# One decoder layer on one core: other banks for the first projection, token tiles in pairs, a third gate buffer, spread compressed-branch steps

## The chip, the core and the metric

The kernel runs on one core of a Trainium2 chip. The metric is the device time of one execution in microseconds, here the median of three runs. The engines are named as in the profile: PE (TensorE, the matrix engine; PEld are its weight loads), DVE (VectorE), ACT (ScalarE), POOL (GpSimd) and SP (SyncE, which issues most DMAs here). The kernel names eight PSUM banks, in which TensorE adds up its products.

## What is computed

One layer of a hybrid decoder on x of 512 tokens by 1024 channels, in fp32. Cut to its frame:

```python
h = rms_norm(x, norm1_g)
u = h @ w_in                       # 11512 columns, split among what follows
(dq, dk, dv, iq, ik, iw, nq, nkv, ng, sz, sxbc, sdt, mg) = split(u)
y_a = dsa_mixer(norm(dq), norm(dk), dv, iq, ik, iw)   # attention to the 256 keys that an index picks
y_b = nsa_mixer(norm(nq), *nkv, sigmoid(ng), ...)     # compressed + selected + window attention
y_c = ssd_mixer(sz, sxbc, sdt, ...)                   # Mamba-2: conv, chunked scan, gated norm
gates = sigmoid(mg)                                   # three gates per channel
mix = gates[0] * (y_a @ w_br_dsa) + gates[1] * (y_b @ w_br_nsa) + gates[2] * (y_c @ w_br_ssd)
x = x + mix @ w_out
x = x + square(relu(rms_norm(x, norm2_g) @ w_ff1)) @ w_ff2
```

DSA scores every earlier key with a small index and keeps the best 256 by repeated MAX8 and MATCH_REPLACE rounds on VectorE. NSA has two key groups and three parts: 31 compressed blocks of the keys (whose probabilities also pick four blocks of 64 keys), the picked blocks, and the window.

## The kernel before

Every fp32 operand of a projection is split into a high and a low half in fp32r, and each product is three matmuls, high by high, high by low and low by high (`mm3`, L455 to L457). A weight block of 128 x 1024 goes through a pipeline (`WS`): a DMA into `wraw` (three buffers), ACT makes the high half `whi` (L172), and DVE or POOL subtracts it for the low half `wlo` (L174). The set `LOWP` says which of the numbered blocks take POOL; before, they are block 0 and blocks 8 to 23. Blocks 0 to 3 belong to the first projection, 4 to 11 to the NSA keys and values, 12 to 19 to the DSA queries.

Two generators share TensorE. `filler()` runs what is plain matmul: the first projection c0 (DSA key and value, index queries and keys, SSD time steps), nkv (two halves, 512 and 304 columns), the DSA queries dq, then z, x (with the conv), the NSA queries nq, 24 merge gates (each written to DRAM as `g_d`), then the branches a0, c0, c1, b0, b1, b2, then `w_out` and the feed-forward part. `main()` runs the mixers: the DSA index, DSA attention, the SSD, NSA. Each step of `main` yields a debt in time, and as much filler is put in behind it. The framework then lists the instructions of each engine by priority and by its own timeline, so the order that an engine runs is not that of the text. The engines run in order; an instruction waits for its semaphores, and all behind it on that engine wait too.

PSUM has eight banks: two named `pj` (projections), two `sc` (scores), two `pT` (transposes), one `pv`, one `pF`. A projection by token tile (`proj_tok`, L473) takes one `pj` bank for each of four tiles of 128 tokens, runs through the four weight blocks, and hands the bank to a callback `cb` that reads it out. For c0 (L695) the callback copies to `u0`, makes the value halves (`make_v`, L547 to L549, tile `v_d`) and the index queries `iqs`; for nkv (L730, L745) it makes `v_s` and `v_w` and copies the keys to `u1` and `u2`, from which `make_k` computes squares (`sqk`, L522), their sum (`stk`, L524), the power on POOL (`rtk`, L527) and the keys.

The SSD runs 16 units (four chunks by four groups). Each unit loads `E` and `xz` by DMA; POOL masks `E`, scales `xt`, `xw` and `xz`, adds `t` and decays the state `hst`; TensorE ends the unit with the transposes of `yv` (L1321), and `yev` is stored to DRAM as `yc_d`. The filler beside it is the conv projections x and then nq, whose queries are stored (`q_d`), and whose norm is a power on POOL (`rs`, L619, `mhalf` as exponent).

NSA has eight (block, group) pairs, and each has four attention steps: j = 0 and 1 by window (w) and selected (s). A step can load something for later. The compressed part of the next pair is done in three pieces (`cmp_a`, which loads the queries `qu` by DMA from POOL and computes the compressed scores at L1032, `cmp_b`, `cmp_c`), hung on the steps of the pair before: `cmp_a` on (0, w), `cmp_b` on (0, s), `cmp_c` on (1, s).

In `branches()` each output tile m of a branch has a gate tile `gld` (two buffers, L1393), loaded from `g_d` by SP, multiplied with the projection's bank (L1508) and added to `mixf` (L1511); in b2 `mixf` is then split into `mixh` and `mixl` (L1513, L1514). For the branches c the gate is first multiplied by a row of factors R (`rtok`). The inputs of a branch come from DRAM through a ring of two tiles (`yr`, L810) that the gates `gth` share, and are split into `yh` (L811) and `yl`.

## Time and profile before

| | |
|---|---|
| median of three runs | 1391.43 us (1391.18 to 1393.15) |
| the profiled execution | 1393.32 us, its span 1391.6 us |
| PE busy | 1361.1 us, 98% |
| PEld | 1134.0 us, 81% |
| DVE | 1002.0 us, 72% |
| ACT | 721.3 us, 52% |
| POOL | 282.0 us, 20% |
| mean granted TensorE clock | 0.994 |

The span is from the first to the last instruction of the profiled execution; the time around it is 1.7 us. Busy time is what an engine spends on instructions, idle time is put down to what released the next one. The granted clock is a share of 2.4 GHz, so 0.50 is 1.2 GHz. A matmul's printed length contains a tail that overlaps with the next one; the pace is read from the starts, or from a busy stretch by its count.

### The profile page before, as it was taken

How to read it: one execution, taken by the hardware profiler on the slowest of the kernel's cores; microseconds unless marked ns; L12 is line 12 of the kernel's file. 1: busy time of each engine (PE TensorE's matmuls, PEld its weight loads, DVE VectorE, ACT ScalarE, POOL GpSimd, SP SyncE). 2: the span in 40 equal slices, each digit the busy share in tenths (PEclk: the TensorE clock that was granted, in tenths of full speed). 3: DMA queues.
4: the chain of work that ended last, by engine and by line, in shares of the span. 5: the costliest groups of instructions: out<-in, count | busy, mean ns of one | idle time of the engine just before them, and what ended most of it. 6: DMA issues, size and time to landing. Idle time of an engine off the chain costs nothing.

```text
span 1391.6 us, 19651 instructions
## 1 busy us (share of the span) xinstructions
PE 1361.1 (98%) x6875; PEld 1134.0 (81%) x6875; DVE 1002.0 (72%) x1966; ACT 721.3 (52%) x1434; POOL 282.0 (20%) x231
## 2 busy tenths in 40 slices
PE   8989999999999999999999999999999999999998
PEld 7878888888877778788887888787889888888887
DVE  6599977999868666477667888878845576767841
ACT  5545336667766757356566564655324434343430
POOL 2345211110048485100000003123100101102000
PEclk9999999999999999999999999999999999999999
DMA  6335654644477696634434544535545665746531
GB/s 194 94 93 145 176 172 133 167 112 126 118 240 240 187 273 193 176 106 137 129 111 140 144 125 118 143 116 162 166 148 152 121 167 134 167 120 134 157 114 53
DMA packets 222592, 205.34 MB, mean 148 GB/s; under 512 B 15369, under 2 KB 169885, under 8 KB 222494
## 3 DMA queue, kind: packets, MB, share of 16 engines
q1 hardware_dynamic: 206524, 180.49, 44.2%
q0 software_dynamic: 15232, 20.98, 8.1%
q10 hardware_dynamic: 738, 2.63, 0.5%
q8 instruction: 54, 0.88, 0.3%
q14 instruction: 44, 0.36, 0.1%
HBM read 167.56 MB, written 36.51 MB: 147 GB/s over the span
## 4 chain that ended last, share of the span: by engine, by line
PE 69%; DVE 10%; DMA 8%; POOL 5%; issue 4%; ACT 3%; SPq 0%; ACTq 0%; POOLq 0%; DVEq 0%
PE pj L455 16%; PE pj L456 16%; PE pj L457 16%; PE sc L455 3%; PE sc L456 3%; PE sc L457 3%; PE pT L935 2%; DMA gld<-g_d 2%; PE sc L897 2%; PE sc L896 1%; DMA yr<-yc_d 1%; PE pv L948 1%; PE pv L947 1%; POOL mixf L1511 1%; DVE mask L867 1%
## 5 line engine op out<-in xcount | busy, mean ns | idle before, releaser
L172 ACT ACTIVATE whi<-wraw 128x1024 fp32r<-128x1024 f32 (+2 forms) x190 | 198.0, 1048 | 226.2 <-PE pj L456 115.5
L174 DVE TENSOR_TENSOR wlo<-wraw,whi 128x1024 fp32r<-128x1024 f32 (+1 forms) x173 | 217.4, 1261 | 101.5 <-ACT whi L172 99.5
L457 PE MATMUL pj<-hTh,wlo 128*128 128x512 f32 x384 | 154.0, 401 | 0.0
L455 PE MATMUL pj<-hTh,whi 128*128 128x512 f32 x384 | 153.5, 400 | 0.2 <-DVE cacc L828 0.2
L456 PE MATMUL pj<-hTl,whi 128*128 128x512 f32 x384 | 153.0, 398 | 0.0
L905 ACT ACTIVATE p<-p,nb,rs 128x256 f32<-128x256 f32 (+3 forms) x192 | 123.2, 645 | 56.2 <-DVE nb L903 56.1
L455 PE MATMUL pj<-whi,hTh 128*128 128x512 f32 (+2 forms) x352 | 138.2, 393 | 6.5 <-DVE stk L525 3.2
L456 PE MATMUL pj<-wlo,hTh 128*128 128x512 f32 (+2 forms) x352 | 138.1, 393 | 0.0
L457 PE MATMUL pj<-whi,hTl 128*128 128x512 f32 (+2 forms) x352 | 137.0, 390 | 0.0
L455 PE MATMUL pj<-yh,whi 128*128 128x512 f32 (+1 forms) x288 | 107.6, 377 | 3.3 <-ACT yh L811 2.3
L456 PE MATMUL pj<-yl,whi 128*128 128x512 f32 (+1 forms) x288 | 107.7, 374 | 0.0
L457 PE MATMUL pj<-yh,wlo 128*128 128x512 f32 (+1 forms) x288 | 107.6, 374 | 0.0
L456 PE MATMUL pj<-h2l,whi 128*128 128x512 f32 (+1 forms) x256 | 96.3, 376 | 0.0
L457 PE MATMUL pj<-h2h,wlo 128*128 128x512 f32 (+1 forms) x256 | 96.2, 376 | 0.0
L455 PE MATMUL pj<-h2h,whi 128*128 128x512 f32 (+1 forms) x256 | 96.1, 376 | 0.0
L991 POOL DMA_DIRECT2D qu<-q_d x32 | 23.6, 738 | 317.1 <-PE sc L897 212.3
L455 PEld LDWEIGHTS pj<-hTh,whi 128*128 128x128 f32 x384 | 72.7, 189 | 15.2 <-issue 1.1
L457 PEld LDWEIGHTS pj<-hTh,wlo 128*128 128x128 f32 x384 | 72.7, 189 | 14.8 <-issue 0.7
L456 PEld LDWEIGHTS pj<-hTl,whi 128*128 128x128 f32 x384 | 72.7, 189 | 13.8 <-issue 0.2
L455 PEld LDWEIGHTS pj<-whi,hTh 128*128 128x128 f32 x352 | 67.0, 190 | 20.5 <-issue 5.7
L939 ACT ACTIVATE pth<-pT 128x512 fp32r<-128x512 f32 x95 | 54.4, 593 | 52.0 <-PE pT L935 51.3
L457 PEld LDWEIGHTS pj<-whi,hTl 128*128 128x128 f32 x352 | 67.0, 190 | 13.1 <-issue 0.7
(385 smaller groups left out, 3280.7 us busy)
## 6 DMA issues: line engine op xcount, KB each, us to landing
wraw<-in_w_in_dram SPq DMA_DIRECT2D x84, 512.0 KB, 4.3
wraw<-in_w_ff_dram SPq DMA_DIRECT2D x58, 512.0 KB, 4.2
gld<-g_d SPq DMA_DIRECT2D x40, 256.0 KB, 2.7
qd<-in_w_ff_dram POOLq DMA_DIRECT2D x18, 512.0 KB, 6.0
q_d<-qev SPq DMA_DIRECT2D x64, 128.0 KB, 3.2
qu<-q_d POOLq DMA_DIRECT2D x32, 256.0 KB, 4.0
E<-ac_d SPq DMA_DIRECT2D x16, 512.0 KB, 5.8
xz<-xz_d SPq DMA_DIRECT2D x16, 512.0 KB, 4.9
```

Source lines behind the costliest of these rows:

```text
L172: act.activation(hi[:, :m], r[:, :m], AF.Copy)
L174: (pool if i in LOWP else dve).tensor_tensor(lo[:, :m], r[:, :m], f(hi[:, :m]), op=ALU.subtract)
L455: pe.matmul(o, lh, rh, start=first, stop=False)
L456: pe.matmul(o, lh, rl, start=False, stop=False)
L457: pe.matmul(o, ll, rh, start=False, stop=last)
L867: dve.scalar_tensor_tensor(wk, r[:, :n], iwt[:, b, h:h + 1], caus[:, 384 - 128 * b:] if h == 0 else wk, op0=ALU.mult, op1=ALU.add)
L896: pe.matmul(s_[:, h % w, :n], u.q[h], kh[:, :n], start=True, stop=False)
L897: pe.matmul(s_[:, h % w, :n], u.q[h], kl[:, :n], start=False, stop=True)
L905: act.activation(u.p[h][:, :n], u.p[h][:, :n], AF.Exp, bias=u.nb[:, h:h + 1], scale=rs8[:, u.b, u.h0 + h:u.h0 + h + 1], accum_out=u.sm[:, ...
L935: pe.transpose(pt[:, h], u.p[h][:, kb * 128:kb * 128 + 128], ident)
L939: act.activation(ph, ptf, AF.Copy)
L991: pool.dma_start(q.rearrange("p (i a) c -> p i (a c)", i=2), src)
```

## The change

Five edits:

- `LOWP` leaves out blocks 14 to 16, so that their low halves are made by DVE.
- `proj_tok` can take the token tiles in pairs: two tiles go through two weight blocks each before the next two blocks. Both halves of nkv use it; the first projection c0 stays with tile after tile, but takes the banks `pj`, `pj`, `sc`, `sc` for its four tiles.
- In NSA the queries of the next pair are loaded at (0, w), `cmp_a` moves to (0, s), `cmp_b` to (1, w), and `cmp_c` stays at (1, s). The mark `nsa0`, for which b0 waits, moves with `cmp_b`.
- In `branches` every third gate tile of the branches b takes the row R, which is not read any more by then, and loads are issued one or two tiles earlier.
- For the branches c the product of gate and R is issued after the first 12 of a tile's 24 matmuls, not ahead of them.

```diff
-LOWP = {0} | set(range(8, 24))
+LOWP = {0} | set(range(8, 14)) | set(range(17, 24))
...
-    def proj_tok(plan, lh, ll, cb):
+    def proj_tok(plan, lh, ll, cb, pair=False, tags=("pj",) * NB):
...
+        if pair:
+            seq = [(t, s) for t0 in (0, 2) for s0 in (0, 2) for t in (t0, t0 + 1) for s in (s0, s0 + 1)]
+        else:
+            seq = [(t, s) for t in range(NB) for s in range(4)]
+        acc = {}
+        for t, s in seq:
+            if s == 0:
+                acc[t] = ps(tags[t], [128, 512])
...
-        yield from proj_tok(P["c0"], hTh, hTl, cb0)
+        yield from proj_tok(P["c0"], hTh, hTl, cb0, False, ("pj", "pj", "sc", "sc"))
...
-            yield from proj_tok(P["nkv"][0], hTh, hTl, cb1)
+            yield from proj_tok(P["nkv"][0], hTh, hTl, cb1, True)
...
-            yield from proj_tok(P["nkv"][1], hTh, hTl, cb2)
+            yield from proj_tok(P["nkv"][1], hTh, hTl, cb2, True)
...
-            if i < len(order) and order[i] not in Q:
+            if i < len(order):
+                b, g = order[i]
+                load(i)
+                yield from cmp_a(b, g, Q[b, g], ratio)
...
+        def load(i):
+            if i < len(order):
                 b, g = order[i]
                 Q[b, g] = [load_q(4 + 2 * g + j, b) for j in range(2)]
-                yield from cmp_a(b, g, Q[b, g], ratio)
+            return iter(())
...
                     elif j == 0 and kind == "w":
-                        u.load = lambda i=i: start(i + 1)
+                        u.load = lambda i=i: load(i + 1)
...
                     if i and j == 0 and kind == "s":
+                        u.load = lambda i=i: cont(i + 1, cmp_q)
+                    if i and j == 1 and kind == "w":
                         u.load = lambda i=i: cont(i + 1, cmp_b)
-                    if i == 4 and j == 0 and kind == "s":
+                    if i == 4 and j == 1 and kind == "w":
                         u.load = lambda i=i: mark(cont(i + 1, cmp_b))
...
-                g_ = bp.tile([128, S], F32, name="gld", bufs=2)
+                if br[0] == "b":
+                    gcnt[0] += 1
+                g_ = R if br[0] == "b" and gcnt[0] % 3 == 0 else bp.tile([128, S], F32, name="gld", bufs=2)
...
                     load_g(8 * bi + m + 2)
+                    load_g(8 * bi + m + 4)
+                elif br == "b0":
+                    load_g(8 * bi + m + 2)
...
-                if br[0] == "c":
-                    dve.scalar_tensor_tensor(th, th, 1.0, R, op0=ALU.add, op1=ALU.mult)
...
-                        yield from proj_ch(P["br_" + br][m], lambda i: yh[i], lambda i: yl[i], p)
+                        for i_, v_ in enumerate(proj_ch(P["br_" + br][m], lambda i: yh[i], lambda i: yl[i], p)):
+                            yield v_
+                            if i_ == 1 and br[0] == "c":
+                                dve.scalar_tensor_tensor(th, th, 1.0, R, op0=ALU.add, op1=ALU.mult)
```

How many filler matmuls stand where follows from the two generators, so these edits move work on every engine. Three places of the emitted order follow.

PE in the first projection, before, from the last matmuls of tile t=1 (`pj`) to the first of t=2; L424 are transposes of x:

```order
L455 MATMUL pj<-whi,hTh 128x456
L456 MATMUL pj<-wlo,hTh 128x456
L457 MATMUL pj<-whi,hTl 128x456
L424 MATMUL pT<-ident,x_125 128x128 x8
L455 MATMUL pj<-whi,hTh 128x456
L456 MATMUL pj<-wlo,hTh 128x456
```

and after, the same place:

```order
L455 MATMUL pj<-whi,hTh 128x456
L456 MATMUL pj<-wlo,hTh 128x456
L457 MATMUL pj<-whi,hTl 128x456
L455 MATMUL sc<-whi,hTh 128x456
L456 MATMUL sc<-wlo,hTh 128x456
L424 MATMUL pT<-ident,x_125 128x128 x4
L457 MATMUL sc<-whi,hTl 128x456
```

The first matmuls of t=2 moved ahead of the transposes and write to a bank of `sc`.

DVE at the end of nkv's second half, before, from `v_w` of tile t=2 to that of t=3 (309 and 310 are the two key groups):

```order
L549 TENSOR_TENSOR v_w_310<-pj,v_w_310 128x64
L873 MATCH_REPLACE mask_628<-m_753,mask_628 128x256
L872 MAX m_762<-mask_628 128x8
L873 MATCH_REPLACE mask_628<-m_762,mask_628 128x256
L872 MAX m_771<-mask_628 128x8
L522 TENSOR_TENSOR sqk<-u_792 128x256
L755 TENSOR_SCALAR gate<-gate 128x192
L873 MATCH_REPLACE mask_628<-m_771,mask_628 128x256
L549 TENSOR_TENSOR v_w_309<-pj,v_w_309 128x64
```

and after:

```order
L879 MATCH_REPLACE mask_640<-m_748,mask_640 128x256
L555 TENSOR_TENSOR v_w_310<-pj,v_w_310 128x64
L174 TENSOR_TENSOR wlo<-wraw,whi 128x1024
L878 MAX m_762<-mask_640 128x8
L174 TENSOR_TENSOR wlo<-wraw,whi 128x1024
L528 TENSOR_TENSOR sqk<-u_786 128x256
L761 TENSOR_SCALAR gate<-gate 128x192
L555 TENSOR_TENSOR v_w_309<-pj,v_w_309 128x64
```

Two of the three subtractions that came over from POOL stand between the two, and fewer rounds of MAX and MATCH_REPLACE.

POOL from the end of the SSD to the first query loads of NSA, before (L1294 ends a unit's sum, L1358 is the SSD's norm, L619 the norm of a half of the queries):

```order
L1275 TENSOR_TENSOR xt<-xz,sv_dth 128x512
L1294 TENSOR_TENSOR t_5475<-t_5475,xz 128x512
L1282 TENSOR_TENSOR xz<-xz,dskip 128x512
L1294 TENSOR_TENSOR t_5541<-t_5541,xz 128x512
L1358 TENSOR_TENSOR rst<-sst,mhalf 128x4
L619 TENSOR_TENSOR rs_319<-ssq,mhalf 128x4x8
L991 DMA qu<-q_d_3_68 128x2x256 x2
```

and after:

```order
L1311 TENSOR_TENSOR t_5475<-t_5475,xz 128x512
L625 TENSOR_TENSOR rs_319<-ssq,mhalf 128x4x8
L1292 TENSOR_TENSOR xt<-xz,sv_dth 128x512
L1299 TENSOR_TENSOR xz<-xz,dskip 128x512
L1311 TENSOR_TENSOR t_5541<-t_5541,xz 128x512
L1375 TENSOR_TENSOR rst<-sst,mhalf 128x4
L997 DMA qu<-q_d_3_68 128x2x256 x2
L997 DMA qu<-q_d_0_65 128x2x256 x2
L625 TENSOR_TENSOR rs_319<-ssq,mhalf 128x4x8
L997 DMA qu<-q_d_2_67 128x2x256 x2
```

Both powers `rs` moved against their neighbours: the first now stands ahead of the last unit's `xt`, the second behind four query loads. The stretch from the SSD's first matmul to its last `yv` transpose holds 335 filler matmuls before and 239 after. By the intervals between the `yv` transposes of one unit and the next these are, before: 38 up to the first, then 13, 15, 11, 15, 14, 17, 24 (intervals 1 to 7), 70 (8), 14, 13, 18, 15 (9 to 12), 17, 17, 24; after: 41, then 8, 15, 10, 11, 13, 17, 13, then 21, then 5, 5, 8, 11, then 16, 21, 24. From there to the first compressed score stand 61 before and 40 after.

## Rows read from the trace of the kernel before

**Rows 1.** The page, part 1: busy us (share of the span) and instructions of each engine.
```profile
PE 1361.1 (98%) x6875; PEld 1134.0 (81%) x6875; DVE 1002.0 (72%) x1966; ACT 721.3 (52%) x1434; POOL 282.0 (20%) x231
```

**Rows 2.** Waits of PE: line and tile, releaser: us in total, times, longest.
```profile
PE pj L455 <- DVE stk L525: 3.2, 1, 3.2
...
PE pj L455 <- DVE gld L1508: 0.9, 3, 0.3
```

**Rows 3.** Stretches: length, busy us (count) by engine, granted clock, DMA share, GB/s.
```profile
core 0: us, PE busy (x) PEld busy (x) DVE busy (x) ACT busy (x) POOL busy (x), PEclk, DMA share, GB/s
27.58:30.99 3.41, 3.41 (x11) 2.97 (x10) 0.71 (x2) 0.00 (x0) 0.00 (x0) 0.50 0.37 99
75.00:100.00 25.00, 21.85 (x123) 19.08 (x122) 24.79 (x62) 12.29 (x28) 11.71 (x6) 1.00 0.30 86
398.70:553.10 154.40, 146.16 (x793) 116.23 (x791) 105.80 (x124) 104.22 (x281) 104.56 (x81) 0.99 0.76 234
417.80:477.00 59.20, 54.67 (x314) 43.80 (x312) 47.43 (x57) 40.76 (x120) 42.27 (x33) 1.00 0.74 226
497.60:530.00 32.40, 32.22 (x180) 25.01 (x179) 19.80 (x26) 19.22 (x57) 32.40 (x25) 1.00 0.90 276
740.00:760.00 20.00, 17.70 (x91) 14.99 (x90) 11.55 (x35) 10.62 (x23) 0.72 (x1) 0.91 0.58 171
935.00:965.00 30.00, 28.28 (x140) 22.36 (x139) 24.09 (x70) 17.74 (x40) 8.79 (x5) 1.00 0.47 144
1100.00:1375.00 275.00, 275.00 (x1215) 227.72 (x1214) 181.38 (x199) 108.27 (x120) 24.23 (x20) 1.00 0.56 137
```

**Rows 4.** PE's timeline at six waits: start, length, instruction, count, [idle before, releaser].
```profile
26.37 0.45 PE L455 MATMUL pj<-whi,hTh 128*128 128x456 f32 x1 [1.80 <-DVE v_d L549]
...
90.51 0.47 PE L455 MATMUL pj<-whi,hTh 128*128 128x512 f32 x1 [3.15 <-DVE stk L525]
...
569.79 0.30 PE L1032 MATMUL sc<-kc,qu 128*128 128x64 f32 x1 [1.33 <-DMA qu<-q_d]
...
753.28 0.73 PE L455 MATMUL pj<-yh,whi 128*128 128x512 f32 x2 [2.30 <-ACT yh L811]
...
885.54 0.63 PE L1032 MATMUL sc<-kc,qu 128*128 128x64 f32 x4 [1.50 <-DMA qu<-q_d]
...
1007.39 0.47 PE L455 MATMUL pj<-whi,mixh 128*128 128x512 f32 x1 [1.80 <-ACT mixh L1513]
```

**Rows 5.** DVE's timeline: a subtraction at 23.30, then 82.85 to 90.76.
```profile
23.30 1.22 DVE L174 TENSOR_TENSOR wlo<-wraw,whi 128x1024 fp32r<-128x1024 f32 x1
...
82.85 0.41 DVE L873 MATCH_REPLACE8 mask<-m,mask 128x256 f32<-128x256 f32 x1
83.29 0.43 DVE L872 MAX8 m<-mask 128x8 f32<-128x256 f32 x1
83.63 2.54 DVE L522 TENSOR_TENSOR sqk<-u 128x256 f32<-128x256 f32 x1
86.10 2.42 DVE L755 TENSOR_SCALAR gate<-gate 128x192 f32<-128x192 f32 x1
...
90.35 0.41 DVE L522 TENSOR_TENSOR sqk<-u 128x256 f32<-128x256 f32 x1
```

**Rows 6.** POOL's timeline: weights 14 to 16, then the SSD and its end.
```profile
81.11 7.29 POOL L174 TENSOR_TENSOR wlo<-wraw,whi 128x1024 fp32r<-128x1024 f32 x3 [7.95 <-ACT whi L172]
...
509.30 5.89 POOL L619 TENSOR_TENSOR rs<-ssq,mhalf 128x32 f32<-128x32 f32 x1
...
554.78 5.43 POOL L619 TENSOR_TENSOR rs<-ssq,mhalf 128x32 f32<-128x32 f32 x1
562.12 2.94 POOL L991 DMA_DIRECT2D qu<-q_d  x4 [1.91 <-ACT gth L776]
```

**Rows 7.** ACT's timeline ahead of the branch a0.
```profile
741.29 0.58 ACT L776 ACTIVATE gth<-pj 128x512 f32<-128x512 f32 x1
...
752.60 1.27 ACT L811 ACTIVATE yh<-yr 128x512 fp32r<-128x512 f32 x2 [4.55 <-DMA yr<-ya_d]
```

**Rows 8.** DVE's timeline at the last pair of b2.
```profile
1006.87 0.76 DVE L1508 SCALAR_TENSOR_TENSOR gld<-gld,pj 128x256 f32<-128x256 f32 x2 [0.36 <-DMA gld<-g_d]
```

More of the change, by code (lines that the diff above doesn't have):

```diff
@@ L472, in run_later @@
                 e[1]()
-    def proj_tok(plan, lh, ll, cb):
+    def proj_tok(plan, lh, ll, cb, pair=False, tags=("pj",) * NB):
         idx, n = plan
-        for t in range(NB):
-            p = ps("pj", [128, 512])
-            for s in range(4):
-                wh, wl = ws.get(idx[s])
-                for k2 in range(2):
-                    k = 2 * s + k2
-                    sl = (slice(None), k, slice(t * 128, t * 128 + 128))
-                    mm3(p[:, :n], lh[sl], ll[sl], wh[:, k2, :], wl[:, k2, :], k == 0, k == KT - 1)
-                if t == NB - 1:
-                    ws.free(idx[s])
-                yield 6 * n / 2.4
-            run_later()
-            with tc.high_priority(offset=0):
-                cb(t, p)
+        if pair:
[6 more added lines that the diff above has]
+                acc[t] = ps(tags[t], [128, 512])
+            wh, wl = ws.get(idx[s])
+            for k2 in range(2):
+                k = 2 * s + k2
+                sl = (slice(None), k, slice(t * 128, t * 128 + 128))
+                mm3(acc[t][:, :n], lh[sl], ll[sl], wh[:, k2, :], wl[:, k2, :], k == 0, k == KT - 1)
+            if t == NB - 1:
+                ws.free(idx[s])
+            yield 6 * n / 2.4
+            if s == 3:
+                run_later()
+                with tc.high_priority(offset=0):
+                    cb(t, acc.pop(t))
     def proj_ch(i, rh, rl, p, first=True, last=True):
@@ L1108, in start, with cmp_q @@
         def start(i):
-            if i < len(order) and order[i] not in Q:
+            if i < len(order):
[4 more added lines that the diff above has]
+            if i < len(order):
                 b, g = order[i]
                 Q[b, g] = [load_q(4 + 2 * g + j, b) for j in range(2)]
-                yield from cmp_a(b, g, Q[b, g], ratio)
+            return iter(())
+        def cmp_q(b, g, ratio):
+            yield from cmp_a(b, g, Q[b, g], ratio)
         def cont(i, part):
@@ L1161, in nsa_units @@
                     elif j == 0 and kind == "w":
-                        u.load = lambda i=i: start(i + 1)
+                        u.load = lambda i=i: load(i + 1)
                         if i == 1:
-                            u.load = lambda i=i: att2(start(i + 1))
+                            u.load = lambda i=i: att2(load(i + 1))
                     if i and j == 0 and kind == "s":
+                        u.load = lambda i=i: cont(i + 1, cmp_q)
+                    if i and j == 1 and kind == "w":
                         u.load = lambda i=i: cont(i + 1, cmp_b)
-                    if i == 4 and j == 0 and kind == "s":
+                    if i == 4 and j == 1 and kind == "w":
                         u.load = lambda i=i: mark(cont(i + 1, cmp_b))
@@ L1376, in branches @@
         th_ = {}
+        gcnt = [0]
         BR = ("a0", "c0", "c1", "b0", "b1", "b2")
```

## The prediction

> **What bounds the kernel now.** I read the busy times first: TensorE is busy 1361.1 of 1391.6 us, and no other engine is near that [rows 1]. So the time is TensorE's own work plus about 30 us in which it waits, plus what a low granted clock costs. The change leaves the matmuls as they are, 6662 in both programs, so it can move the end only through waits and the clock; the order of the two programs tells where, the trace what each place costs. The view of waits lists 20 kinds on TensorE, and the largest is 3.2 us in all [rows 2]: nothing big can be removed, the sum is one of small terms, and each is read at its own place. Two prices are needed for all. In the late stage, where TensorE never waits, 1215 matmuls take 275.00 us, so a matmul of the filler, 512 columns, is 0.226 us [rows 3]. A wait costs a little more than its printed idle time: the matmul after the wait at 26.37 lasts 0.45 us, where 456 columns at that pace are 0.20, so I add 0.2 a wait [rows 4].
>
> **First projection (c0).** Token tile t=2 needs a bank that tile 0 still holds: 1.80 us of idle until VectorE's `v_d`. Right behind it TensorE's granted clock is 0.50, that is 1.2 GHz, for 3.41 us, which is 1.7 us lost [rows 3, 4]. With tiles 2 and 3 in the `sc` banks, which nothing else holds there, the order puts the first matmul of t=2 directly behind t=1, and the transposes of x move in among them. Wait 2.0 and clock 1.7: −3.7. If the clock falls at that place anyway, −2.0.
>
> The Trainium skill ("TensorE: Matmul & The Clock Gate", section "Why this matters for your kernels") says that it is one long idle gap which drops TensorE to half rate. The trace has a longer wait that is followed by no drop, 3.15 us before 90.51, with clock 1.00 over 75 to 100 [rows 3, 4], so it is not the length alone. By the page the short c0 gap should not be what drops the clock, c0 would give 2.0 and the whole sum would be 1.7 smaller; I book what the rows show.
>
> **Keys and values (nkv) and the three weights.** GpSimd computes the low halves of weights 14 to 16 in 7.29 us from 81.11 [rows 6]. VectorE operations that start beside it last as long as its own pieces: `sqk` 2.54 us against 0.41 later, the gate's scaling 2.42, though it is no bigger [rows 5]. `v_w` of the last tile stands behind both on VectorE, it holds the bank of dq's t=1, and TensorE waits 3.15 us [rows 4]. The change puts three subtractions of 1.22 us on VectorE: +3.7, less 2.1 and 2.0 of stretch. In the changed order three MAX8 and three MATCH_REPLACE fewer stand before `v_w`, each about 0.4 [rows 5]: another 2.4. So `v_w` is ready some 2.9 earlier and that wait nearly goes: −3.2. Against it, GpSimd's subtraction of weight 13 now comes directly after that of weight 12, ahead of the small `rtk`, where `sqk` and `v_s` of nkv's first half are due: one such stretch is 2.1 by the same rows. Taken as −3.2 + 1.7 = −1.5, with ends −3.4 and 0. The pairing itself I cost at nothing: the emitted order keeps pairs for the first two tiles of nkv's first half only, the other six come tile after tile as before, and weights are there in time in both.
>
> **SSD.** This is the largest unknown. Up to the SSD the changed program consumes filler faster, and between the SSD's first matmul and its last `yv` transpose it holds 239 filler matmuls where 335 stood: 96 × 0.226 = 21.7 us less cover. In 398.70 to 553.10 TensorE waits 154.40 − 146.16 = 8.2 us already [rows 3]. I take it by the intervals between one unit's transposes and the next's, in the counts that stand with the order above. Intervals 1 to 7, 417.8 to 477.0, lose 22: 5.0 us of cover where TensorE was busy 54.67 of 59.20. GpSimd was busy only 42.27 there, 6.0 a unit, so it doesn't set the pace and what waits is a chain through several engines; if that chain is as long as before, all 5.0 come back as waits, if TensorE was part of it, none. Half: 2.5. Interval 8, 477.0 to 497.6, held 70 because a conv was late; the conv now comes earlier and 21 remain, 9.5 us of work, more than any unit needs: 0. Intervals 9 to 12, 497.6 to 530.0, hold 29 for 60. TensorE was busy 32.22, without 60 × 0.226 = 13.6 that is 18.6, with 29 it is 25.2. GpSimd was busy all 32.40, of which 5.89 is the power function `rs` [rows 3, 6], which moves away: 26.5. So it lacks 1.3. `rs` now stands ahead of the last unit's `xt`, among intervals with as much filler as before; a small part of it may show: 0.7. Sum +4.5. Ends: −2 (the waits shrink with the late conv gone) and +13 (5.0, the old 32.4 for intervals 9 to 12, which is 7.2, and the 0.7).
>
> **SSD to NSA.** Between the last `yv` transpose and the first compressed score stand 40 filler matmuls for 61: 4.7 us less cover in front of queries that TensorE already waits 1.33 for [rows 4]. But on GpSimd the second `rs` (5.43 us from 554.78) moves behind the first four `qu` loads, of which the first went out only at 562.12 [rows 6]; the wait of 1.91 for a gate tile in front of that load may stay. +2, ends −1.5 and +4.7.
>
> **The branch a0.** TensorE waits 2.30 for `yh`, and the clock of 740 to 760 is 0.91, that is 1.8 us [rows 3, 4]. From the last gate's `gth` at 741.29 to `yh` at 752.60 the chain of a shared ring and DMA is 11.3 us [rows 7] and unchanged; the order puts about 1.4 us more TensorE work under it. So −1.2 (ends 0 and −4, with the clock).
>
> **Spread compressed steps.** The queries of the next unit are loaded one step before their scores, so the 1.50 at 885.54 goes: −1.7 [rows 4]. The load is issued by GpSimd, which does nothing else there. Attention runs ahead of c1 afterwards, and from 935 to 965, where TensorE idles 1.72 in several waits, the order has no attention in c1's last part [rows 3]: −2.3. What is late next is b0: the first `yh` pair of b0 comes from a ring of two and may keep TensorE 1.5. Together −0.8 (ends −2.5 and +1).
>
> **Third gate buffer.** The last pair of b2 waits 1.80; the page names `mixh`, but VectorE's `gld` at 1006.87 held the bank and itself waited 0.36 for the gate's load [rows 4, 8]. Three smaller waits on `gld` come to 0.9 [rows 2]. With a third buffer the load stands a pair of output tiles earlier in the order. −2.5, ends −1 and −2.9. The product for c now follows 12 matmuls, 2.7 us, instead of the start; a projection has 24, so it is hidden, and if it weren't it would cost its own 0.7.
>
> **Sum.** −3.7 − 1.5 + 4.5 + 2 − 1.2 − 1.7 − 0.8 − 2.5 = −4.9. The profiled execution took 1393.32 (span 1391.6), so it would take 1388.4; it lies 1.9 over the median of the runs, 1391.43, and I forecast the median: 1386.5.
>
> **Rivals.** (1) *SSD loses its cover.* Both groups of intervals keep the old pace and the queries are late: +13 and +4.7 against −11.4 from all else: +6.3, 1397.7. It decides from +14.2 for the two places, beyond which the kernel is more than 0.2% slower. For it: GpSimd was busy in every microsecond of 497.6 to 530.0. Against: without `rs` it has about as much to do as TensorE there, and in the earlier intervals neither was full. (2) *The front gives back what it gained.* Weight 13's subtraction and weight 17's hold both `sqk`, so the wait at dq moves to nkv: 0 for −1.5; the clock falls at another place than c0: −2.0 for −3.7; the gates' wait goes to the next load, −1. Sum −4.9 + 1.5 + 1.7 + 1.5 = −0.2, and 1391.2, no difference. (3) *SSD loses nothing.* The lost filler had nothing to cover but the late conv, and the queries come as early as the work before them: 0 in place of +4.5 and +2, and the clock at a0 stays up: −4.9 − 6.5 − 1.8 = −13.2, so 1378.2. For it: in intervals 9 to 12 TensorE hardly waited, so filler there may only have lengthened them. (4) *The change doesn't do what it says*: true for the pairing, which is priced at nothing, so it moves no number.
>
> **How the numbers follow.** My forecast, 1380 to 1388.6: 0.42. Rival 3, below that: 0.17. Rival 2, within 0.2% (2.8 us, about what a measurement of this kernel can tell from none): 0.22. Rival 1 and anything above 1394.2: 0.19. So faster 0.59, same 0.22, slower 0.19. For 8 in 10 the range takes in rival 2 whole and most of rival 3: 1377 to 1395; rival 1's upper part and rival 3's lower are left out.
>
> **What would show it.** Right: no wait above 0.5 on `v_d` or at dq's second tile, clock 1.00 over 25 to 50, no wait of compressed scores on `qu` after the first unit, no wait on `gld` or `mixh`. Wrong: the idle time in the SSD and up to the first compressed score exceeds the former 8.2 + 1.3 by over 10, which makes rival 1; `sqk` of 2.5 us and TensorE waiting for `v_s` around 68, which makes rival 2; or new low-clock stretches of 3.4 us behind waits that were harmless before.

## The result, and the profile after

The changed kernel takes 1377.73 us (median of four runs, 1375.92 to 1380.26) beside 1392.29 for the kernel before on the same chip: a ratio of 0.9884, with a 95% interval of 0.9862 to 0.9906 (estimated from all the runs; the quotient of the two medians is 0.9895). Two later measurements of the same instruction order gave 0.9921 (0.9901 to 0.9941) and 0.9899 (0.986 to 0.9938), which by their medians are 13.1 and 14.2 us less than the kernel before. Single executions of some kernels took 2239 to 6063 us, and every time in this document leaves them out. The forecast was a gain of 4.9 us to 1386.5; the gain is about 14. The time lies inside the range, near its lower end and on rival 3 (1378.2), but the size of the change was missed by a factor of nearly three.

The profiled execution took 1380.26 us, span 1378.5, granted clock 0.997, against 1393.32, 1391.6 and 0.994 before: 13.1 less. The page of the changed kernel, part 1:

```profile
PE 1357.1 (98%) x6875; PEld 1131.5 (82%) x6875; DVE 1002.4 (73%) x1969; ACT 722.5 (52%) x1434; POOL 262.9 (19%) x228
```

TensorE has the same 6875 instructions and still bounds the kernel. Its waits in the changed kernel (line and tile, releaser: us in total, times, longest):

```profile
PE pv L1286 <- DVE E L1297: 2.6, 3, 1.8
PE pj L455 <- DVE v_s L555: 2.2, 1, 2.2
PE pT L1315 <- DVE hst L1321: 2.1, 1, 2.1
...
PE pT L1338 <- DVE yv L1332: 1.8, 3, 0.7
PE pj L455 <- ACT yh L817: 1.8, 2, 1.2
...
PE sc L1038 <- DMA qu<-q_d: 0.8, 1, 0.8
PE pj L455 <- DVE rtok L1532: 0.7, 1, 0.7
PE pj L455 <- DVE gld L1532: 0.4, 1, 0.4
```

Of the waits in [rows 2] and [rows 4], those on `v_d` (1.80), at dq's second tile (3.15), on `qu` in the later units (1.50) and on `mixh` (1.80) are gone. `v_s` is new in size (2.2 for 0.2). Gates are still waited for: the third tile, which is the row R (`rtok`, 0.7), and `gld` (0.4 and a smaller one of 0.2).

The span can be cut into seven stretches that end at the same events in both programs: first matmul of nkv, first of DSA attention, first of the SSD, last `yv` transpose, first matmul of a0, first of `w_out`, end. The stretches of the kernel before that [rows 3] doesn't hold already (columns as there):

```profile
1.90:39.00 37.10, 34.59 (x159) 29.37 (x159) 23.14 (x46) 21.49 (x42) 6.36 (x11) 0.91 0.58 183
39.00:187.40 148.40, 143.83 (x754) 119.20 (x753) 131.50 (x290) 67.88 (x139) 56.95 (x33) 1.00 0.49 132
187.40:398.70 211.30, 211.06 (x1071) 176.43 (x1070) 177.03 (x391) 133.79 (x271) 21.78 (x29) 1.00 0.51 138
...
553.10:740.20 187.10, 185.71 (x943) 155.57 (x941) 121.80 (x333) 105.44 (x224) 13.64 (x12) 0.99 0.47 131
740.20:1007.40 267.20, 259.26 (x1384) 218.07 (x1382) 214.06 (x512) 148.46 (x310) 46.13 (x30) 0.99 0.48 140
1007.40:1391.60 384.20, 380.50 (x1784) 319.07 (x1784) 227.97 (x264) 139.79 (x169) 31.31 (x28) 1.00 0.53 134
```

and all seven of the changed kernel:

```profile
1.90:35.60 33.70, 33.56 (x147) 27.92 (x148) 22.92 (x45) 19.94 (x38) 6.03 (x10) 1.00 0.65 200
35.60:193.60 158.00, 155.79 (x819) 130.82 (x819) 135.78 (x307) 72.61 (x147) 49.09 (x31) 1.00 0.54 144
193.60:404.40 210.80, 210.53 (x1074) 176.22 (x1073) 177.13 (x388) 137.38 (x275) 22.02 (x30) 1.00 0.50 134
404.40:536.70 132.30, 123.98 (x680) 97.26 (x679) 89.42 (x107) 91.65 (x263) 102.14 (x82) 0.97 0.79 241
536.70:743.80 207.10, 206.30 (x1072) 173.27 (x1071) 142.27 (x392) 125.69 (x271) 14.12 (x13) 1.00 0.48 132
743.80:993.60 249.80, 246.04 (x1307) 206.97 (x1306) 204.94 (x455) 133.54 (x271) 36.89 (x28) 1.00 0.51 146
993.60:1378.50 384.90, 380.87 (x1786) 319.00 (x1784) 229.24 (x267) 141.52 (x171) 31.32 (x28) 1.00 0.52 134
```

The lengths don't compare, because filler moved between stretches (the SSD has 680 matmuls for 793). What compares is TensorE's idle time, length minus PE busy, and the stretches at half clock, 3.41 us each, which cost 1.7 apiece and sit in the busy time. Four of those lie in the execution of before (at 27.6 [rows 3], 409.9, 570.3, 754.6) and two in that of after (448.4, 506.4), the first 15 us left out. Worked out from the rows, in us:

| stretch | idle before | idle after | difference | half clock | together | forecast |
|---|---|---|---|---|---|---|
| c0 | 2.51 | 0.14 | −2.37 | −1.7 | | |
| nkv to DSA attention | 4.57 | 2.21 | −2.36 | 0 | −6.4 with c0 | −5.2 |
| DSA attention to SSD | 0.24 | 0.27 | 0 | 0 | 0 | 0 |
| SSD | 8.24 | 8.32 | +0.1 | +1.7 | +1.8 | +4.5 |
| SSD end to a0 | 1.39 | 0.80 | −0.6 | −1.7 | −2.3 | +2 |
| a0 to `w_out` | 7.94 | 3.76 | −4.2 | −1.7 | −5.9 | −6.2 |
| `w_out` and after | 3.70 | 4.03 | +0.3 | 0 | +0.3 | 0 |
| sum | 28.6 | 19.5 | −9.1 | −3.4 | −12.5 | −4.9 |

The other 0.6 of the 13.1 is spread over the busy time. So two thirds of the gain is idle time that is gone, from the front and from the branches, a quarter is the clock, and two places where losses were forecast lost little or nothing.

### The profile page after: what moved, and what is told of

Same layout as the page of the kernel before. It is cut to its first block, busy times and chain, and to the rows that moved or that the text cites. A ratio compares the mean times of both kernels' runs of the same rounds, so it can differ in the third digit from the quotient of the medians.

```text
span 1378.5 us, 19656 instructions
## 1 busy us (share of the span) xinstructions
PE 1357.1 (98%) x6875; PEld 1131.5 (82%) x6875; DVE 1002.4 (73%) x1969; ACT 722.5 (52%) x1434; POOL 262.9 (19%) x228
## 4 chain that ended last, share of the span: by engine, by line
PE 82%; DVE 5%; DMA 4%; POOL 4%; ACT 3%; issue 2%; SPq 0%; POOLq 0%; DVEq 0%; ACTq 0%
PE pj L455 19%; PE pj L457 19%; PE pj L456 19%; PE sc L457 3%; PE sc L455 3%; PE sc L456 3%; PE pT L941 3%; PE sc L903 2%; PE sc L902 2%; PE pv L953 2%; PE pv L954 2%; DMA E<-ac_d 1%; DMA gld<-g_d 1%; POOL t L1311 1%; ACT E L1290 1%
## 5 line engine op out<-in xcount | busy, mean ns | idle before, releaser
L174 DVE TENSOR_TENSOR wlo<-wraw,whi 128x1024 fp32r<-128x1024 f32 (+1 forms) x176 | 230.4, 1312 | 95.3 <-ACT whi L172 94.0
L455 PE MATMUL pj<-whi,hTh 128*128 128x512 f32 (+2 forms) x336 | 131.5, 391 | 2.2 <-DVE v_s L555 2.2
L456 PE MATMUL pj<-wlo,hTh 128*128 128x512 f32 (+2 forms) x336 | 131.9, 393 | 0.0
L457 PE MATMUL pj<-whi,hTl 128*128 128x512 f32 (+2 forms) x336 | 131.1, 390 | 0.0
L455 PEld LDWEIGHTS pj<-whi,hTh 128*128 128x128 f32 x336 | 63.7, 190 | 15.5 <-DVE v_s L555 2.5
L457 PEld LDWEIGHTS pj<-whi,hTl 128*128 128x128 f32 x336 | 63.9, 190 | 11.9 <-issue 0.8
```

Source lines behind the costliest of these rows:

```text
L174: (pool if i in LOWP else dve).tensor_tensor(lo[:, :m], r[:, :m], f(hi[:, :m]), op=ALU.subtract)
L455: pe.matmul(o, lh, rh, start=first, stop=False)
L456: pe.matmul(o, lh, rl, start=False, stop=False)
L457: pe.matmul(o, ll, rh, start=False, stop=last)
```

## The experiments

The questions were: is the gain the sum of its parts, or do front (banks, weights, pairs) and back (spread steps, gate edits) need each other; does filler that leaves the SSD cost waits there (the forecast) or was it no cover (rival 3); and what releases the first query load of NSA. All times are medians, and each ratio is against runs of the kernel before on the same chip. A difference between two experiments is that of their medians; where the ratios give clearly another one, it is told as well.

### Front alone, back alone, and two single edits

Front alone is the kernel before with these edits; back alone is the changed kernel with these three undone:

```diff
-LOWP = {0} | set(range(8, 24))
+LOWP = {0} | set(range(8, 14)) | set(range(17, 24))
...
-        yield from proj_tok(P["c0"], hTh, hTl, cb0)
+        yield from proj_tok(P["c0"], hTh, hTl, cb0, False, ("pj", "pj", "sc", "sc"))
...
-            yield from proj_tok(P["nkv"][0], hTh, hTl, cb1)
+            yield from proj_tok(P["nkv"][0], hTh, hTl, cb1, True)
```

(the last for both halves). Then the `LOWP` line alone, and the c0 line alone.

> The kernel before with the three edits of the front alone: weights 14 to 16 on VectorE, the sc banks for c0, the pairs for nkv. The SSD then holds 239 filler matmuls as in the changed kernel (335 before). Theory A, the excess over the forecast comes from the front, because filler that it moves ahead of the SSD was no cover there: c0 -2.7, nkv and dq -3.4, SSD 0, the way from the SSD to NSA -2.7, so about -9 us (ratio 0.9935), and TensorE's idle time between the SSD's first matmul and its last yv transpose stays at 8 us. Rival B, the front gives only the waits that it removes itself and the excess belongs to the later edits: -5 us (0.9965). Rival C, the lost filler was cover, and only the later edits make up for it: 0 to +5 us, with over 12 us of idle in the SSD.

> The kernel before with the two later edits alone: the spread compressed steps and the third gate buffer with its earlier loads and later product. The filler in the SSD stays at 335. Theory A: the waits behind the first NSA unit and on gates, and a part of a0, -5 us (0.9965). Rival B: the excess belongs here: -9 us (0.9935). Rival C: as in the changed kernel less the loss of the front, -13 us or more (0.990).

> The kernel before with weights 14 to 16 on VectorE and nothing else. The SSD holds 270 filler matmuls for 335, and its interval 8 has 23 for 70. Theory A: the wait of 3.2 at dq goes, SSD idle stays at 8 us: -3 to -5 us (0.997). Rival C: 65 fewer at 0.226 are 14.7 us of cover, of which half comes back as waits: +3 us or more (1.002).

> The kernel before with the sc banks for tiles 2 and 3 of the first projection and nothing else. The SSD holds 270 filler matmuls as well. Theory A: the wait of 2.0 and the low clock behind it go, SSD idle stays at 8 us: -3 to -4 us (0.9975). Rival C: +3 us or more. If the clock falls somewhere else in place of 27.6, -2 us.

| | time | ratio (95%) | idle a0 to `w_out` | filler in the SSD |
|---|---|---|---|---|
| front alone | 1387.12 | 0.9964 (0.995 to 0.9977) | 9.90 | 239 |
| back alone | 1389.02 | 0.998 (0.9963 to 0.9997) | 4.80 | 335 |
| `LOWP` alone | 1396.54 | 1.0031 (1.0014 to 1.0047) | 11.12 | 270 |
| c0 alone | 1395.42 | 1.0027 (1.0011 to 1.0044) | 12.26 | 270 |

The kernel before took 1392.06 beside them (35 runs). The idle column comes from one row each, first matmul of a0 to first of `w_out`, in this order front, back, `LOWP`, c0:

```profile
735.30:1000.50 265.20, 255.30 (x1360) 215.24 (x1358) 212.27 (x492) 143.44 (x297) 42.42 (x29) 0.99 0.48 140
...
738.10:998.90 260.80, 256.00 (x1368) 214.70 (x1367) 212.92 (x502) 144.11 (x304) 42.15 (x30) 1.00 0.49 143
...
749.90:1010.60 260.70, 249.58 (x1304) 206.76 (x1302) 203.25 (x460) 135.16 (x273) 45.55 (x28) 0.99 0.47 141
...
749.80:1009.60 259.80, 247.54 (x1303) 205.73 (x1301) 202.13 (x460) 135.27 (x273) 46.68 (x28) 1.00 0.48 141
```

Each single edit takes away its own wait (with the c0 banks TensorE idles 0.03 of the first 37.10 us, 2.51 before) and is slower all the same: the branches idle 11.1 and 12.3 us where they idled 7.94. The size is what rival C named (+3 or more), but not the place: the SSD idles 9.9 and 9.1, 1.7 and 0.9 more than before, where half of 14.7 was to come back. Front alone gains 4.9 in all, which is rival B's number and not theory A's −9, but gives 2.0 back in the branches; its SSD idles 9.2, near the 8 of theory A and not the 12 of rival C. Back alone gains 3.0, less than any of its three expectations. Their sum, 7.9, is short of the whole change (13.1 to 14.6 by the medians above, 11 to 16 by the ratios). The parts are not additive, which the gate edits show once more below: an edit in the first 100 us changes how much filler is left for each later place, and so the waits there. Why the branches wait more when filler comes earlier is not settled: less attention stands beside them (1303 to 1360 matmuls in the stretch for 1384), but the changed kernel has 1307 there and idles least.

### The changed kernel again, and without one edit at a time

Without pairs: `True` left out in both calls for nkv. Without gate edits: the code of before for `gld` (two buffers, no row R, loads not issued earlier) and for the product for c. Without spread: `cmp_a`, `cmp_b`, `cmp_c` hung on the steps of before; the third gate buffer stays.

> The changed kernel itself once more, on the same chip and in the same rounds as the next three, since the two halves alone gave 0.9964 and 0.9980 and their sum is 0.994. Theory A, the halves need each other (filler moved ahead leaves more of the branches without attention beside them, which then wait for gates and yh unless the later edits help): 0.989 to 0.991, -13 us. Rival D, the first figure of 0.988 was a lucky chip: 0.994, -8 us.

> The changed kernel without the pairs for nkv. Theory A, pairs are kept in the order for two tiles only and carry nothing: as e5 within 3 us. Rival E, the pairing decides the front: a wait of some 3 us comes back at dq's second tile and the gain over the kernel before falls to -8 us or less.

> The changed kernel with two gate buffers, the old lookahead and the old place of the product for c. Up to the branch c0 the order is that of the changed kernel. Theory A: waits on gld (0.9, 1.2, 0.6) and on mixh (2.0) come back as in e1, +4 to +5 us against e5. Rival F, the gates are a small term there too: +2.5 us, the forecast's own price, or less.

> The changed kernel with the old steps for the compressed part. Theory A: attention and branches shift against each other as in e1, with waits of 1.5 and 2.5 on gates and yh around 880 to 890, +3 to +4 us against e5. Rival F: the forecast's price for it alone, +0.8, or the removed 1.7.

> The kernel of e8 once more for its trace, since the profiled execution of e8 was disturbed. Theory A: the waits that the spread steps remove are not those on qu (1.5) alone; with the old steps a0 starts earlier and the branches run with more attention beside them until later, and TensorE waits on yh and gates around 880 to 900 for 4 us more than in e5. Rival F: one wait of about 1.7 on qu and nothing else.

| | time | ratio (95%) | the edit's worth by medians | by ratios |
|---|---|---|---|---|
| changed kernel | 1378.77 | 0.9921 (0.9901 to 0.9941) | | |
| without pairs | 1381.57 | 0.993 (0.9911 to 0.995) | 2.8 | 1.3 |
| without gate edits | 1385.8 | 0.9957 (0.994 to 0.9974) | 7.0 | 5.0 |
| without spread | 1382.52 | 0.9945 (0.9925 to 0.9965) | 3.8 | 3.3 |

The trace without spread is that of one more execution (1379.99), which the median doesn't contain. Between the whole and the kernel without gate edits the intervals hardly meet, and the slowest run of the one (1382.45) is faster than the fastest of the other (1383.61), so a worth of 5 to 7 stands; the other two are less sure, since those intervals overlap. By its ratio the changed kernel lies between theory A (0.989 to 0.991) and rival D (0.994), by its median at theory A's −13. Without pairs it stays within the 3 us of theory A. Without gate edits it lost more than either expectation, without spread about what theory A said.

The gate edits can be read directly, since the stretch from a0 to `w_out` starts at the same time and has the same 1308 matmuls with and without them. With them, then without:

```profile
742.60:991.80 249.20, 245.37 (x1308) 207.08 (x1306) 205.43 (x455) 133.56 (x271) 36.92 (x28) 1.00 0.50 147
```

```profile
742.60:999.40 256.80, 248.91 (x1308) 207.93 (x1306) 201.06 (x458) 135.05 (x273) 43.11 (x28) 0.99 0.48 143
```

It is 7.6 us longer without, 7.89 − 3.83 = 4.1 in idle time, the rest in the busy time, of which 1.7 is a stretch at half clock (949.3). The clock is lower over all runs without them, too: 0.9941 on average for 0.9962, by the same estimate as below about 2.9 us. Among the waits without the gate edits:

```profile
PE pj L455 <- ACT yh L817: 3.1, 3, 2.3
PE pj L455 <- DVE gld L1525: 2.4, 4, 1.0
PE pj L455 <- ACT mixh L1530: 1.8, 1, 1.8
```

With them the waits on `yh` are 2.1 in all, and on gate tiles 1.4. In the new order, then, more hangs on the gate loads than the waits that [rows 2, 4] named for gates (`gld` 0.9, `mixh` 1.8): 4.1 in idle time, and about twice the 2.7 or more in all. Without spread the stretch idles 259.60 − 253.10 = 6.50 instead of 3.83, most of it where theory A put it: between 860 and 900 TensorE waits 2.3 for `yh` and 1.2 for `gld`, and no wait on `qu` came back behind the first unit.

### Does filler cover the SSD?

No run was made for this alone; all of them answer it, because the number of filler matmuls in the SSD differs from kernel to kernel. TensorE's idle time by the intervals of the prediction, each kernel's own first SSD matmul and `yv` transposes as bounds:

| filler in the SSD | kernels | 1 to 7 | 8 | 9 to 12 | whole SSD |
|---|---|---|---|---|---|
| 335 | before, back, `rt4` moved in before | 4.5, 4.2, 6.8 | 1.0 | 0.2, 0.5, 0.7 | 8.2, 7.6, 11.2 |
| 270 | `LOWP`, c0 | 3.3, 3.7 | 1.6, 1.8 | 2.5, 1.7 | 9.9, 9.1 |
| 245 | no pairs | 7.6 | 0.7 | 2.4 | 11.9 |
| 239 | after, after again, front, no gates, no spread, `rt4` moved in after, weight 12 moved | 5.1, 6.3, 5.0, 4.8, 4.8, 4.2, 4.6 | 0 | 2.6, 2.9, 3.0, 3.5, 3.2, 2.7, 2.7 | 8.3, 10.1, 9.2, 10.4, 10.1, 7.4, 8.0 |

With 96 filler matmuls more or less the whole SSD idles 9.0 on average in one order and 9.1 in the other, and executions of one order differ by 3 and more among themselves. Part of that is the clock: of the executions with 335 and 239, those that idle 8.3 or less have one or two stretches at half clock in the SSD, the others none. The length contains both. It is 154.4, 154.1 and 156.2 with 335, and 132.3, 132.2, 130.8, 132.6, 131.8, 131.2 and 132.8 with 239: on average 22.9 us less, where the filler that left is 96 × 0.226 = 21.7. So the stage got shorter by all of the filler's own time. In intervals 1 to 7 the removed filler covered nothing. In 9 to 12 it covered some: about +2.5 on average, while GpSimd's busy time fell from 32.40 [rows 3] to 26.44, mostly by the move of `rs`. The rows of after, 1 to 7 and 9 to 12:

```profile
420.00:477.50 57.50, 52.40 (x304) 41.63 (x303) 41.27 (x50) 38.76 (x115) 44.10 (x37) 0.97 0.78 237
...
486.40:514.00 27.60, 25.05 (x128) 17.78 (x128) 19.05 (x21) 18.33 (x55) 26.44 (x22) 0.94 0.83 249
```

The gains that level it are interval 8 (1.0, the late conv) and the part ahead of the first transposes, which idles 1.94 in before (398.7 to 417.8) and 0.11 in after (404.4 to 420.0). Taking filler out of the SSD with all else in place wasn't tried, since the list is made anew with each edit; what `rs` and the late conv gave is known by intervals only.

### What releases the first query load of NSA

The page put the 1.91 us in front of the load [rows 6] on a gate tile. The other candidate was the small tile `rt4` of the SSD's norm: it lay in the SSD's pool, the pool's space goes to the queries, and the store from it (`rs_d`) had to land first. The edit moves it to the pool of constants, in the kernel before and in the changed one; the instruction order of both stays the same.

```diff
-        rt = sp.tile([4, 128], F32, name="rt4")
+        rt = cp.tile([4, 128], F32, name="rt4")
```

> The kernel before, with the 4 x 128 tile from which the SSD's norm factors are stored (rt4) in the pool of constants instead of the SSD's pool. The order is the same on every engine. Theory G: in the kernel before the first NSA queries were loaded at 562.1, 1.9 us after GpSimd's power had ended, because their tiles lie where the SSD's pool lay and so wait for the store of the norm factors to land; with rt4 elsewhere the load goes out at 560.2 to 560.5, when the power ends, the wait of 1.3 at the second compressed score goes and, if nothing else lets the clock fall there, 1.7 more: -1.5 to -3 us. Rival H: it waits for a gate tile, as the profile's row names: the load stays at 9.1 us after the last yv transpose and nothing changes.

> The same move of rt4 in the changed kernel, whose order also stays the same. Theory G: there the power stands behind the load, so the load goes out when the SSD's last other store has landed; the trace of the changed kernel names the store of the norm factors as releaser, 7.2 us of idle on GpSimd: the load goes out 0.5 to 1.5 us earlier and the wait of 0.8 at the compressed scores shrinks: 0 to -1 us against the changed kernel. Rival H: no change of the load's distance to the last yv transpose (5.2 us).

Before with it: 1391.43, ratio 0.9993 (0.9971 to 1.0014), no difference that the runs resolve; the expected −1.5 to −3 lies within the interval. After with it: 1378.5, ratio 0.9899 (0.986 to 0.9938), the same as after. GpSimd's timeline of the changed kernel, then of before with `rt4` moved:

```profile
533.40 1.02 POOL L1375 TENSOR_TENSOR rst<-sst,mhalf 128x4 f32<-128x4 f32 x1 [3.88 <-DVE sst L1373]
541.66 2.93 POOL L997 DMA_DIRECT2D qu<-q_d  x4 [7.24 <-DMA rs_d<-rt]
545.79 5.45 POOL L625 TENSOR_TENSOR rs<-ssq,mhalf 128x32 f32<-128x32 f32 x1 [1.20 <-DVE ssq L624]
```

```profile
556.10 1.02 POOL L1358 TENSOR_TENSOR rst<-sst,mhalf 128x4 f32<-128x4 f32 x1 [9.25 <-DVE sst L1356]
557.09 5.43 POOL L619 TENSOR_TENSOR rs<-ssq,mhalf 128x32 f32<-128x32 f32 x1
562.76 2.94 POOL L991 DMA_DIRECT2D qu<-q_d  x4 [0.25 <-issue]
```

The trace of after names the store, and with the tile elsewhere the load of before goes out as soon as the power ends, 7.7 us after the last `yv` transposes (555.10) instead of 9.0: the cause is shown. The wait at the second compressed score falls from 1.33 to 0.2. In after the load goes out 0.7 earlier against those transposes, and the wait of 0.8 on `qu` is gone. What this is worth is too small to be seen in the times. The change had it the other way: the power moved behind the loads, and the first load goes out 5.0 us after the last `yv` transposes (536.70) instead of 9.0 (553.10), with the store still in front of it.

### Weight 12 on VectorE too

The largest new wait outside the SSD is `v_s`, 2.2 us. In the changed kernel GpSimd's subtraction of weight 13 comes right behind that of 12 and ends at 65.9, and VectorE's `sqk` beside it is stretched:

```profile
60.39 2.40 POOL L174 TENSOR_TENSOR wlo<-wraw,whi 128x1024 fp32r<-128x1024 f32 x1 [0.51 <-POOL wlo L174]
63.25 2.65 POOL L174 TENSOR_TENSOR wlo<-wraw,whi 128x1024 fp32r<-128x1024 f32 x1 [0.46 <-ACT whi L172]
...
63.58 2.60 DVE L528 TENSOR_TENSOR sqk<-u 128x256 f32<-128x256 f32 x1
66.10 0.21 DVE L555 TENSOR_TENSOR v_s<-pj,v_s 128x64 fp32r<-128x64 f32 x1
```

So the low half of weight 12 is made by VectorE as well:

```diff
-LOWP = {0} | set(range(8, 14)) | set(range(17, 24))
+LOWP = {0} | set(range(8, 12)) | {13} | set(range(17, 24))
```

> The changed kernel with the low half of weight 12 on VectorE too. Theory: the wait of 2.2 for v_s near 64 is there because GpSimd's subtractions of weights 12 and 13 come one right after the other and the second one stretches sqk from 0.4 to 2.6; with weight 12 on VectorE that of weight 13 starts earlier and is over before sqk: sqk 0.4, no wait for v_s over 0.5, and -2 us against the changed kernel (1376.5). Rival: VectorE's 1.2 us more stands ahead of v_s and gives half of it back: -1 or 0.

It takes 1374.58 (four runs, 1374.44 to 1375.35), ratio 0.9868 (0.9829 to 0.9906) to before. That beats the kernel before; beside the changed order run on the same chip (1378.5, 1375.56 to 1383.1) it is 3.9 less, and the runs don't overlap, though the two intervals do, so that it is faster than the change is likely and not settled. The wait on `v_s` explains 2.2 of the 3.9; the rest is not traced. TensorE has no idle time left between c0 and the start of DSA attention:

```profile
34.40:190.00 155.60, 155.60 (x820) 130.87 (x820) 133.86 (x308) 72.70 (x146) 46.75 (x30) 1.00 0.54 147
```

The wait went in another way than expected. VectorE and GpSimd in this kernel:

```profile
59.96 1.23 DVE L174 TENSOR_TENSOR wlo<-wraw,whi 128x1024 fp32r<-128x1024 f32 x1
...
61.50 0.42 DVE L528 TENSOR_TENSOR sqk<-u 128x256 f32<-128x256 f32 x1
...
62.06 2.65 POOL L174 TENSOR_TENSOR wlo<-wraw,whi 128x1024 fp32r<-128x1024 f32 x1 [3.36 <-ACT whi L172]
```

Counted from nkv's first matmul (34.40, and 35.60 in the changed kernel) weight 13's subtraction starts at 27.7 in both. It was `sqk` that moved ahead of it, from 28.0 to 27.1, and lasts 0.42 instead of 2.60. One reason is the operation of VectorE at 61.15 in the changed kernel, a product for the index mask: it started within weight 12's subtraction and lasted 1.92, and lasts 0.48 here.

## Why the prediction was wrong

**c0, and the front as a whole: right, a little small.** `v_d` is gone and no drop stands behind its place. c0 and nkv together gave −6.4 where −5.2 stood; 0.66 of it is a wait for `hTh` at 9.96 in before, which the second profiled execution of the changed kernel has as well (0.47), so that part is not the change's. The first 15 us tell nothing of the clock: their matmuls start 0.38 apart, as at half clock, from 11.6 to 13.5 in before and from 12.1 to 14.7 in after, where the row prints 1.00.

**nkv: right in mechanism, mis-sized.** The dq wait is gone and weight 13 did stretch `sqk` and hold `v_s`, 2.2 for the 1.7 priced. What else was idle up to the start of DSA attention went to zero, so the term is −2.4 and not −1.5. Rival 2's sign, `sqk` of 2.5 and a wait for `v_s` around 68, was seen, and the wait is smaller than the one it replaced. That VectorE's operations beside GpSimd last as long as its pieces was too broad a reading (see the end of the last section). The pairing, costed at nothing, may be worth 2.8; its interval allows nothing as well.

**SSD: the step that failed.** I took lost filler as lost cover: half of 5.0 in intervals 1 to 7. It was none, as rival 3 had it: idle is 4.5 before and 5.1 after, 5.2 and 5.0 on average over the executions in the table. In 9 to 12 the balance of GpSimd (26.5 forecast, 26.44 measured) against TensorE was right, but the term was 2.4 and not 1.3. The 0.7 for `rs` showed nowhere. And I left the two places out that gain, interval 8 (−1.0) and the head (−1.8). In idle time +0.1 against +4.5; by the lengths over all executions the stage lost 22.9 us where its filler is 21.7.

**SSD to NSA: the second step that failed.** Less cover was real, but the first load came 4.0 us earlier after the last unit, and the wait is 0.80 for 1.33 [rows 4]: −0.5, or −2.3 with the half clock that came behind it before, against +2. The wait in front of the load did stay, as I allowed for; I had put it on a gate tile, and it is the store of `rt4`.

**a0, spread, gates: the sum right, by errors that cancel in part.** −5.9 for −6.2. a0's wait for `yh` (2.30 [rows 4]) is gone entirely, where I counted 1.2. The gates were bounded at 2.9 by the waits of the old order; in the new order taking them back costs 4.1 in idle time and 5 to 7 in all. Without them the stretch idles 7.89 in the new order, as much as in the kernel before (7.94), and I had priced that link between front and branches at nothing. The sign "no wait on `gld`" came only in part (`rtok` 0.7, `gld` 0.6). So the worth of an edit read off the trace of before is its worth in that order only.

**The clock: mis-sized.** I booked 1.7 for c0 and none elsewhere. It came out at −3.4 in this pair of executions. One pair could be luck, since the places change from execution to execution (see the last section), but the runs agree with it: the mean granted clock is 0.9937 over 64 runs of the kernel before, and 0.9961 over the 14 of the changed order. As an estimate, with 1 minus the clock as the lost share of the span, that is 8.8 us against 5.4. Where the clock falls is no property of the order; how much of it is lost on average is.

**The price of a wait.** The 0.2 that I added to a wait set a printed length, with its tail, against a pace. By the starts it is 0.1: the matmul at 26.37 is followed by the next at 26.66, where 0.20 is the pace. This moves c0 and spread by 0.1 each.

**The weighing of the rivals.** Rival 3 named what happened, and I gave it 0.17. Its ground for intervals 9 to 12 held in part only, since filler did cover 2.5 there. Against my forecast the profile already held a hint. Filler that stands ahead of a unit's matmul in TensorE's order can lie on the unit's chain and lengthen it; then the stage gets shorter by the filler's time when it leaves, as it did here. That is the end "none" of my term. I took half for want of a row, but there was one: the intervals of before hold different amounts of filler. From 1 to 7 these are 13, 15, 11, 15, 14, 17 and 24 matmuls, and the idle times 0, 1.06, 1.10, 0, 0, 0.93 and 1.43 us. The first and the seventh:

```profile
417.77:425.57 7.80, 7.80 (x48) 6.23 (x47) 7.80 (x11) 5.27 (x16) 4.75 (x4) 1.00 0.85 258
465.08:476.99 11.91, 10.48 (x60) 8.25 (x60) 7.14 (x9) 9.10 (x27) 3.25 (x3) 1.00 0.53 159
```

More filler didn't go with less idle time. Seven intervals of different length are a hint and no proof.

## What to carry to other kernels

Filler beside a chain of small dependent steps is cover only if the chain is late without it: where no engine is full, ask whether the stage gets shorter by the filler's own time when it leaves. The waits of a trace bound an edit's worth in that order alone; where a scheduler lists all anew, run the edit inside the new order and take it out again there, since a single good edit can be slower (+4.5 and +3.4 here) and two halves worth 4.9 and 3.0 made 13 to 15 together here. A releaser that the trace names for a load may hide another with the same end: what shares the memory with the loaded tile is a candidate.

## What the hardware showed that was not expected

**Where the clock drops changes from execution to execution.** The kernel with `rt4` moved has the instruction order of before. Its wait of 3.15 us ahead of dq's second tile is the one of [rows 4], which was followed by full clock; here it was followed by half clock. The wait, and the stretch behind it:

```profile
89.12 0.77 PE L455 MATMUL pj<-whi,hTh 128*128 128x512 f32 x1 [3.15 <-DVE stk L525]
```

```profile
88.60:92.01 3.41, 2.88 (x7) 2.34 (x8) 3.41 (x10) 1.14 (x3) 2.81 (x2) 0.50 0.38 141
```

In turn this execution shows no drop at 27.6, behind the same wait on `v_d` (1.79). The changed kernel dropped at 448.4 and 506.4, behind waits of 2.05 and 1.84; its second profiled execution had waits of 0.72 and 2.11 at these places, and no drop at all after the start. The drops of the first:

```profile
448.39:451.80 3.41, 3.41 (x8) 1.77 (x7) 1.91 (x3) 3.17 (x12) 3.41 (x3) 0.50 0.81 205
506.40:509.83 3.43, 3.43 (x10) 2.02 (x10) 3.43 (x5) 0.72 (x1) 3.42 (x2) 0.50 0.89 209
```

Four drops against two make 3.4 us between one pair of executions, of the order of the forecast itself. A term for the clock at one place, read from one execution, is a guess; the average over many runs (0.9937 and 0.9961 above) is not. The Trainium skill ("TensorE: Matmul & The Clock Gate", section "Why this matters for your kernels") puts a drop down to one long idle gap. Here drops followed waits of 1.33 and 1.80 [rows 4] and of 2.05 us, 2.11 was followed by none, and the same 3.15 was followed by one in one execution and by none in another, so the length of the gap alone doesn't decide.

**GpSimd's subtraction stretched some of VectorE's operations that started within it, and not others.** `sqk` lasts 0.42 when it starts at 61.50, 0.56 us ahead of the subtraction, and 2.60 when it starts within one: 2.2 us on the critical path by the order of two instructions. In the kernel with weight 12 on VectorE these two start within the subtraction from 62.06 to 64.71:

```profile
62.36 0.42 DVE L530 TENSOR_REDUCE stk<-sqk 128x4 f32<-128x256 f32 x1
...
62.83 1.91 DVE L531 TENSOR_SCALAR stk<-stk 128x4 f32<-128x4 f32 x1
```

The reduction isn't stretched, while the operation on four columns, 0.17 in the changed kernel, lasts to the subtraction's end. In before MATCH_REPLACE8 and MAX8 at 82.85 and 83.29 [rows 5] start within one as well and last 0.41 and 0.43. So that kernel didn't lose the stretch, it moved it from `sqk`, which held `v_s`, to an operation for which TensorE doesn't wait.
